# The m5 product by seven half-sized products in the middle pairs of a two-level Strassen matmul

## The chip, the cores and the metric

One core of a Trainium2 chip runs the kernel. The core has a matmul engine (TensorE, PE in the profile, with its weight loads shown as PEld), a vector engine (VectorE, DVE), a scalar engine (ScalarE, ACT), GpSimd (POOL, used here only to issue DMAs) and a sync engine (SP, which also issues DMAs). Each takes its own instructions in the order in which they were written, and waits on semaphores for the others. The metric is the device time of one execution in microseconds (us).

## The reference

```python
def setup_inputs():
    m, k, n = 4096, 4096, 4096      # all float32, standard normal

def reference(a, b, bias):
    return np.tanh(np.matmul(a, b) + bias)
```

A 4096 x 4096 x 4096 matrix product, a bias for each column, and tanh.

## The kernel before

**First level.** Data is held as fp16, sums in fp32 in PSUM. The output is cut into blocks of 256 rows by 1024 columns. There are sixteen row blocks and four column blocks c = 0 to 3. One such block is an *item* n. Each item is a 2 x 2 Strassen scheme in the Winograd form with seven products of 128 rows, 512 columns and half of the inner dimension (2048). The left operands are the quarters a11, a12, a21, a22 of the item's rows and the differences s1, s2, s5, s6, s7 of two quarters each. The right operands are the blocks b11, b22 and the sums d1, d3, d4, e6, e7. The products are m2 = s2 b11, m5 = s5 b22, m3 = a11 d3, m1 = s1 d1, m4 = a22 d4, m6 = s6 e6, m7 = s7 e7 (`PRODUCTS`). A whole product is 16 matmuls of 128 x 128 weights by 512 columns (function `whole`).

**Second level.** Two neighbouring items p = n and q = n + 1 use the same right operand. Their two left operands, one above the other, with the inner dimension and the columns halved, are again a 2 x 2 scheme. It has seven products of 8 matmuls with 256 columns each, in place of two whole products (32 matmuls with 512 columns). A product that is taken so I call *by seven halves*. It needs five differences of left halves, called lefts (`left`, tiles `h`, four buffers in turn), on VectorE. Its right operands are two quarters of the first-level operand and five forms d1, d3, d4, e6, e7 made from its quarters. `group0`, `group1` and `group2` issue two, three and two of the seven products (`multiply`). Between them ScalarE copies a part out of PSUM (`third`, tile `x`, one buffer), and VectorE makes one sum (the function that `group0` returns, the middle sum) and two differences (the function that `group1` returns). `seed` writes zeros with ScalarE into a half of a PSUM bank, since these matmuls add to what stands there.

**The stages.** In column block 2 the last eight items and in block 3 the last ten run in pairs, in an order written out by hand (`four`, and `last_four` for the very last pair). I call them four-product pairs, since m2, m3, m4 and m6 are taken by seven halves in them. Block 2 has the first pair, two middle pairs, and the leaving pair, in which m6 is whole because its operands are being replaced for block 3. Block 3 has the first pair, three middle pairs, and the last pair. In the last pair alone m5 is by seven halves too; forms of b22 for it are made during the pairs before (`pull_four` with `M5_AT`, and `twice_right` at the end of `four`). In a first, middle or leaving pair m5, m1 and m7 are whole.

**Queues.** Forms of m2 and m6 lie in DRAM and are loaded through GpSimd's DMA queue (tile `form`). Six buffers go round: when a product has used a form (`let_go`), `pull_four` issues the load of the next one. The quarters of the next pair are fetched on SP's queue from a DRAM copy (`fetch`, a<-scratch), each into the buffer that this pair's quarter leaves. Results are stored from SP as well (`store`). The fp32 tiles `ds` and `s` have two buffers each, `o` has three. PSUM has eight banks: d, c, z and w for p and for q.

**The end of a pair before.** The last whole m7 (of q) is followed by `ds -= z`, the seed of z for the next q, the fetch of a12, the tanh of ds and its store, all written before the next pair's first group.

Of the kernel before, what the change touches and what calls it, by code (L numbers as in the profile page):

```python
# [8 lines left out]
P = 128  # L9
# [72 lines left out]
M5_AT = {"d3": (2, 13), "d4": (3, 13)}  # L82
M5_REST = 3
# [30 lines left out]
def kernel(  # L114
# [84 lines left out]
    def beginning(n):  # L199
        return begins.get(items[n][0], len(items))  # L200
# [560 lines left out]
    free, held, placed, left_count, resting = [], {}, {}, [0], []  # L761

    def pull_four():
        for i in range(len(resting)):
            resting[i][0] -= 1
        while resting and resting[0][0] <= 0:
            free.append(resting.pop(0)[1])
        if queue and free and queue[0][0] == "m5":
            what, name = queue.pop(0)
            tag = free.pop(0)  # L770
            pool = spare if tag == "sum" else bops
            rights[what, name] = pool.tile([P, TP, NB // 2], fp16, name="form", tag=tag)
            twice_right(what, name)
            forms[what, name] = dram.tile([P, TP, NB // 2], fp16, name=f"form_m5_{name}")
            nc.gpsimd.dma_start(out=forms[what, name], in_=rights.pop((what, name)))
            resting.append([M5_REST, tag])
            return
        while queue and free and queue[0][0] != "m5":
            what, name = queue.pop(0)
            tag = held[what, name] = free.pop(0)  # L780
            pool = spare if tag == "sum" else bops
            rights[what, name] = pool.tile([P, TP, NB // 2], fp16, name="form", tag=tag)
            nc.gpsimd.dma_start(out=rights[what, name], in_=forms[what, name])  # L783

    def let_go(n, what, name):
        tag = held.pop((what, name))
        c = items[n][0]
        if c < NC - 1 and not queue and tag != "sum":
# [17 lines left out]
    def pair_of(n, what):  # L806
        return (bank(i, 0, TWO[what][2]) for i in (n, n + 1))
# [26 lines left out]
    def group0(n, what):  # L834
        p, q = pair_of(n, what)
        multiply(n, what, p[:, HALF[1]], "s5", (1, 1))
        multiply(n, what, q[:, HALF[0]], "s2", (0, 0))
# [21 lines left out]
    def whole(n, left_, right, parts=None):  # L859
        at = by_four(aset[n][left_])  # L860
        for to, half in parts or ((bank(n, 0, "z"), ds(0, NB)),):
            for t in range(T):
                nc.tensor.matmul(  # L863
                    to[:, half], at[:, t // TB, t % TB], bop[right, t // TB][:, t % TB, half],
                    start=False, stop=t == T - 1, skip_group_check=True,
                )

    def four_sum(n, name, leave=False, over=None):
# [4 lines left out]
        upper = (n - beginning(n)) % 2 == 0  # L873
        st = aset[n]
        if leave:
            st[name] = wide.tile([P, T, P], fp16, name=name, tag="wide")
        elif over is not None:
            st[name] = st[over] if over in QUADS else bops.tile([P, T, P], fp16, name=name, tag=over)
        elif name == "s7":
            st[name] = st["a12"]  # L880
        elif upper and name in ("s2", "s1", "s6") and (n, name) != (beginning(n), "s2"):
            st[name] = side[:, :, ds(NB if name == "s6" else 0, NB)].rearrange(
                "p a (b m) -> p a b m", m=P
            )
        elif name == "s6":
            st[name] = bops.tile([P, T, P], fp16, name="s6", tag="e6_1")
        else:
            st[name] = sums.tile([P, T, P], fp16, name=name, tag="sum")
        tt(by_four(st[name]), by_four(st[x]), by_four(st[y]), SUB)

    def seed(n, where, half):
        nc.scalar.copy(bank(n, 0, where)[:, HALF[half]], zeros)

    def add21(n):
        st = state.setdefault((n, 0), {})
        st["ds"] = temps.tile([P, NB], fp32, name="ds", tag="ds")
        tt(st["ds"], bank(n, 0, "z"), bias_bc[:, :NB], ADD)

    def add12(n):
        st = state[n, 0]  # L900
        st["s"] = temps.tile([P, NB], fp32, name="s", tag="sc")
        tt(st["s"], bank(n, 0, "z"), bias_bc[:, NB:], SUB)
# [10 lines left out]

    def four(n):
        c = items[n][0]
        p, q, m = n, n + 1, n + 2
        more = m in fours
        leave = not more
        pair = {i: items[i][1][0] for i in (p, q)}

        seed(p, "c", 1)
        seed(q, "c", 0)
        if leave:
            give_back(c, 0)
        w = group0(n, "m4")
        left(n, "m4", "s1")
        w()
        left(n, "m2", "s1")
        w = group0(n, "m2")
        if leave:  # L930
            give_back(c, 1)
        left(n, "m4", "s7")
        w()
        left(n, "m4", "s6")
        w = group1(n, "m4")
        left(n, "m2", "s7")
        w()
        if n > beginning(n):
            four_sum(p, "s5")
        w = group1(n, "m2")  # L940
        left(n, "m2", "s6")
        w()
        if n == beginning(n):
            four_sum(p, "s5")
        group2(n, "m4")
        if leave:
            give_back(c, 5)
        left(n, "m3", "s5")
        group2(n, "m2")
        if leave:  # L950
            give_back(c, 6)
        left(n, "m3", "s2")
        add21(p)
        add12(p)
        w = group0(n, "m3")
        four_sum(p, "s6", leave)
        w()
        add21(q)
        add12(q)
        left(n, "m3", "s1")  # L960
        four_sum(q, "s6", leave)
        fetch(m, "a21")
        if more:
            fetch(m + 1, "a21")
        four_sum(q, "s5")
        if leave:
            give_back(c, 7)
        whole(p, "s5", "b22")
        tt(state[p, 0]["s"], bank(p, 0, "z"), state[p, 0]["s"], SUB)
        for i in (p, q):  # L970
            tt(state[i, 0]["ds"], state[i, 0]["ds"], bank(i, 0, "d"), ADD)
            result(state[i, 0]["ds"], pair[i], 1, c, 0)
        if leave:
            give_back(c, 8)
        w = group1(n, "m3")
        if leave:
            give_back(c, 9)
        if more:
            seed(p, "d", 1)
            seed(q, "d", 0)  # L980
        left(n, "m3", "s7")
        left(n, "m3", "s6")
        w()
        four_sum(p, "s1")
        four_sum(p, "s7", leave)
        fetch(m, "a22")
        fetch(m, "a11")
        if leave:
            fetch(m, "a12")
        whole(q, "s5", "b22")  # L990
        if leave:
            give_back(c, 10)
        tt(state[q, 0]["s"], bank(q, 0, "z"), state[q, 0]["s"], SUB)
        if not leave:
            seed(p, "w", 1)
            seed(q, "w", 0)
        group2(n, "m3")
        if leave:
            give_back(c, 11)
        if not leave:  # L1000
            left(n, "m6", "s5")
            left(n, "m6", "s2")
        for i in (p, q):
            tt(state[i, 0]["s"], bank(i, 0, "c"), state[i, 0]["s"], ADD)
            result(state[i, 0]["s"], pair[i], 0, c, 1)
        four_sum(q, "s1")
        four_sum(q, "s7")
        if more:
            fetch(m + 1, "a22")
            fetch(m + 1, "a11")  # L1010
        whole(p, "s1", "d1")
        if leave:
            give_back(c, 12)
        tt(bank(p, 0, "c"), state[p, 0]["s"], bank(p, 0, "z"), SUB)
        if leave:
            whole(q, "s1", "d1")
            tt(bank(q, 0, "c"), state[q, 0]["s"], bank(q, 0, "z"), SUB)
            give_back(c, 13)
            for i in (p, q):
                whole(i, "s6", "e6", ((bank(i, 0, "c"), ds(0, NB)),))  # L1020
                result(bank(i, 0, "c"), pair[i], 1, c, 1)
                give_back(c, 14 if i == p else 16)
                whole(i, "s7", "e7")
                if i == p:
                    asum(m, "s2")
                tt(state[i, 0]["ds"], state[i, 0]["ds"], bank(i, 0, "z"), SUB)
                nc.scalar.activation(state[i, 0]["ds"], state[i, 0]["ds"], TANH)
                store(state[i, 0]["ds"], pair[i], 0, c, 0)
                give_back(c, 15 if i == p else 17)
            asum(m, "s5")  # L1030
            for k in range(18, 29):
                at_slot(SLOTS * m + k - 18, give_back, c, k)
            return
        w = group0(n, "m6")
# [740 lines left out]
```

## Time and profile before

| | us |
|---|---|
| three runs | 1532.35, 1534.38, 1531.41 |
| their median | 1532.35 |
| the profiled execution | 1531.29 |
| its span, first to last instruction | 1529.6 |

The four-product stages of the profiled execution, by start of each pair:

| column block | first pair | middle pairs | leaving or last pair |
|---|---|---|---|
| 2 | about 929.8 | 974.98, 1020.15 | 1065.32 (leaving, to 1111.3) |
| 3 | 1301.5 | 1346.67, 1391.85, 1437.02 | 1482.19 (last) |

The granted clock of TensorE is full throughout. How to read the views: "busy" is the time in which an engine executes, a share of the span; a matmul's row is longer than its place in the stream, since matmuls overlap, so their price is read from the chain of waits, which merges them into stretches. A row of a timeline has start, length, engine, line, operation, output<-input, shapes, count, and in brackets the idle time before it and what ended it. In rows of DMA issues the last number is the time from issue to landing.

### The profile page before, as it was taken

To read this page: it belongs to the slowest core of one execution; us is meant where nothing else is said; L and a number is where in the kernel's file an instruction comes from. 1 tells how busy PE (TensorE), PEld (TensorE's weight loads), DVE (VectorE), ACT (ScalarE), POOL (GpSimd) and SP (SyncE) were. 2 spreads that over 40 slices of the span, in tenths; PEclk is the share of its full clock that TensorE was granted. 3 is DMA by queue.
4 is the path that set the end of the run, shared out by engine and by line. 5 is a ranking of instruction groups with operands and counts; after the bars stand their busy time and mean duration, and the time that the engine had idled before them with its cause. 6 is when DMAs were issued, how large, how long until landed. Compare 5 with 4: busy or idle time off the path is not lost.

```text
span 1529.6 us, 22760 instructions
## 1 busy us (share of the span) xinstructions
PE 1524.3 (100%) x8541; PEld 834.4 (55%) x8541; DVE 1225.5 (80%) x1641; ACT 337.0 (22%) x677; POOL 475.5 (31%) x860
## 2 busy tenths in 40 slices
PE   9999999999999999999999999999999999999999
PEld 4444444444445666544444556766644555777766
DVE  6789877777987776777798877888669977888898
ACT  3432111111221122111122112222122211222222
POOL 7775543334513231343550121111123001111210
DMA  9999998999979998999996878988979657888984
GB/s 177 183 212 256 279 239 214 229 210 228 192 210 295 265 281 264 240 255 239 221 195 183 278 265 316 331 302 296 322 243 200 186 190 240 307 303 322 326 304 173
DMA packets 205778, 381.39 MB, mean 249 GB/s; under 512 B 25058, under 2 KB 104162, under 8 KB 205668
## 3 DMA queue, kind: packets, MB, share of 16 engines
q0 software_dynamic: 117872, 194.30, 55.8%
q1 hardware_dynamic: 87124, 185.31, 35.6%
q8 instruction: 67, 1.10, 0.3%
q10 hardware_dynamic: 672, 0.33, 0.1%
q14 instruction: 43, 0.35, 0.1%
HBM read 324.01 MB, written 141.56 MB: 304 GB/s over the span
## 4 chain that ended last, share of the span: by engine, by line
PE 95%; issue 2%; DMA 1%; POOL 1%; DVE 0%; ACT 0%; POOLq 0%; DVEq 0%
PE ps L465 58%; PE ps L825 14%; PE ps L863 12%; PE ps L640 6%; PE ps L1424 4%; DMA form<-form_m 1%; DMA land<-in_a_dram 0%; DMA side<-in_b_dram 0%; POOL b L368 0%; POOL land L1465 0%; POOL form L783 0%; POOL side L1513 0%; POOL form_m L725 0%; POOL first L1493 0%; DVE s L144 0%
## 5 line engine op out<-in xcount | busy, mean ns | idle before, releaser
L465 PEld LDWEIGHTS <-s 128*128 128x128 f16 x2256 | 220.8, 98 | 260.2 <-DVE s L144 0.2
L465 PEld LDWEIGHTS <-a 128*128 128x128 f16 x1984 | 194.1, 98 | 230.7
L465 PE MATMUL ps<-b,s 128*128 128x512 f16 x1204 | 274.7, 379 | 0.0
L144 DVE TENSOR_TENSOR s<-a,a 128x2048 f16<-128x2048 f16 (+1 forms) x190 | 228.5, 1208 | 14.0 <-DMA a<-scratch 12.7
L465 PE MATMUL ps<-e,a 128*128 128x512 f16 x964 | 219.7, 379 | 0.0
L465 PE MATMUL ps<-d,a 128*128 128x512 f16 x896 | 202.5, 379 | 0.0
L268 DVE STREAM_TRANSPOSE a<-nat 128x1024 f16<-128x1024 f16 (+2 forms) x202 | 175.0, 909 | 9.9 <-PE ps L465 8.3
L825 PEld LDWEIGHTS <-h 128*128 128x128 f16 x1440 | 140.8, 98 | 27.4 <-issue 0.4
L465 PE MATMUL ps<-d,s 128*128 128x512 f16 x688 | 155.5, 379 | 0.0
L783 POOL DMA_DIRECT2D form<-form_m x119 | 63.0, 529 | 273.1 <-PE ps L825 240.6
L240 POOL DMA_DIRECT2D nat<-in_a_dram x176 | 93.0, 533 | 133.0 <-DVE a L268 58.2
L368 POOL DMA_DIRECT2D b<-in_b_dram x192 | 103.4, 543 | 84.5 <-DVE a L268 31.1
L144 DVE TENSOR_TENSOR a<-a,a 128x2048 f16<-128x2048 f16 x88 | 106.9, 1215 | 0.0
L485 ACT ACTIVATE o<-ps 128x512 f32<-128x512 f32 x94 | 56.4, 600 | 187.1 <-issue 107.0
L825 PE MATMUL ps<-form,h 128*128 128x256 f16 x688 | 83.8, 273 | 0.2 <-DMA form<-form_m 0.2
L640 PEld LDWEIGHTS <-h 128*128 128x128 f16 x680 | 66.5, 98 | 16.7
L725 POOL DMA_DIRECT2D form_m<-stage x15 | 8.2, 548 | 199.9 <-DVE stage L144 199.9
L863 PEld LDWEIGHTS <-s 128*128 128x128 f16 x448 | 43.8, 98 | 47.8
L144 DVE TENSOR_TENSOR ps<-ps,x 128x256 f32<-128x256 f32 x106 | 45.6, 431 | 29.9 <-PE ps L825 18.1
L825 PE MATMUL ps<-d,h 128*128 128x256 f16 x576 | 68.8, 273 | 0.0
L144 DVE TENSOR_TENSOR h<-a,a 128x1024 f16<-128x1024 f16 x99 | 66.4, 683 | 1.4 <-PE ps L825 1.3
L144 DVE TENSOR_TENSOR ps<-cs,ps 128x512 f32<-128x512 f32 x43 | 29.5, 693 | 41.6 <-PE ps L465 40.2
(185 smaller groups left out, 1958.1 us busy)
## 6 DMA issues: line engine op xcount, KB each, us to landing
a<-scratch SPq DMA_DIRECT2D x140, 512.0 KB, 5.4
form<-form_m POOLq DMA_DIRECT2D x119, 512.0 KB, 6.2
out_dram<-o SPq DMA_DIRECT2D x223, 256.0 KB, 5.3
nat<-in_a_dram POOLq DMA_DIRECT2D x288, 128.0 KB, 7.2
scratch<-a SPq DMA_DIRECT2D x48, 512.0 KB, 7.0
b<-in_b_dram POOLq DMA_DIRECT2D x160, 128.0 KB, 6.0
scratch<-a SPq DMA_DIRECT2D x32, 256.0 KB, 6.1
cast<-in_b_dram POOLq DMA_DIRECT2D x64, 128.0 KB, 9.1
```

What stands on the lines that cost most here:

```text
L144: nc.vector.tensor_tensor(out=out_, in0=in0, in1=in1, op=op)
L240: nc.gpsimd.dma_start(out=tl[ds(q * QP, QP), :, :], in_=src.rearrange("(mb p) k -> p mb k", p=QP),)
L268: nc.vector.transpose(dst[:, ds(b0 * tb, n * tb), :].rearrange("P (b t) (mb p) -> P mb b t p", t=tb, p=QP), src[:, :, ds(b0, n), :].rearra ...
L368: nc.gpsimd.dma_start(out=dst[ds(q * QP, QP), ds(t, nt)], in_=src)
L465: nc.tensor.matmul(st[where], at, bt, start=(what == "m2" or n < LEAD and what == "m1") and i == 0, stop=i == len(ts_) - 1, skip_group_che ...
L485: nc.scalar.activation(o, src, TANH)
L640: nc.tensor.matmul(to, at, bt, start=False, stop=t == TP - 1, skip_group_check=True)
L725: nc.gpsimd.dma_start(out=forms[what, name], in_=stage)
L783: nc.gpsimd.dma_start(out=rights[what, name], in_=forms[what, name])
L825: nc.tensor.matmul(to, at, bt, start=False, stop=t == TP - 1, skip_group_check=True)
L863: nc.tensor.matmul(to[:, half], at[:, t // TB, t % TB], bop[right, t // TB][:, t % TB, half], start=False, stop=t == T - 1, skip_group_che ...
L1424: nc.tensor.matmul(mb[m % 4, j], aq[m, kt // T][:, kt % T, :], right(kt, j), start=fresh and kt == k0, stop=stop and kt == k1 - 1, skip_gr ...
```

## The change

In middle pairs m5 becomes a product by seven halves, like m2, m3, m4 and m6. `four` now writes the order of every pair, and `last_four` is gone.

- *Which pairs.* `x` and `y` name the two late products of a pair, x in bank d and y in bank w. In first and middle pairs x is m6 and y is m5; in the leaving and the last pair x is m5 and y is m6. In the first pair y is still whole m5 (`if first`), in the leaving pair both x and y are whole.
- *Forms of b22.* They are made once in the first pair of each block (`form`, `m5_form`) and stay. d4, d1 and d3 get buffers of their own. e6 and e7 are written over two quarters of b22 itself, after the first pair's whole m5. In block 2 these two quarters are moved to DRAM earlier, and back at the start of the leaving pair (`move("m5", ...)`). The forms made by `pull_four` (`M5_AT`) go.
- *Order in a middle pair.* m4 and m2 interleaved, m3's group 0, m6's group 0, m3's group 1, m6's group 1, m3's group 2, whole m1 of q, m6's group 2, m5's group 0, whole m1 of p, m5's group 1, whole m7 of p, m5's group 2, whole m7 of q. Before: m4 and m2 interleaved, m3's group 0, whole m5 of p, m3's group 1, whole m5 of q, m3's group 2, whole m1 of p, m6's group 0, whole m1 of q, m6's group 1, whole m7 of p, m6's group 2, whole m7 of q.
- *Where sums lie.* Differences of quarters are kept in the quarters' own buffers or in two halves A and B of `side` (`home`).
- *Left-over work.* What closes a pair is no longer written at its end. It goes on a list, `left_over`: `close` (`ds -= z` of q, the seed of z, the fetch of a12), then the tanh and store of ds of p, s of p, s of q and ds of q. The next pair takes it off at four places with `more`: the first two entries after m4's group 0, one after m2's group 0, one after m4's group 1, the last after m2's group 1.
- *Full-width work.* `take_d` reads m4 from d with the bias, and z is added later; `take_c` reads c with the bias; `take_z` writes s - z to `o`; `take` adds or subtracts m6 or m5. There are sixteen of these fp32 instructions of 512 columns in a middle pair, as before.

The diff, cut to the routine's middle pair and the functions it calls:

```diff
-M5_AT = {"d3": (2, 13), "d4": (3, 13)}
-M5_REST = 3
...
     def between(n, what):
-        return {
-            "m2": bank(n, 0, "c")[:, HALF[0]], "m4": bank(n + 1, 0, "c")[:, HALF[1]],
-            "m3": bank(n, 0, "w")[:, HALF[0]], "m5": bank(n, 0, "w")[:, HALF[0]], "m6": bank(n + 1, 0, "w")[:, HALF[1]],
-        }[what]
+        i, where, half = {
+            "m2": (n, "c", 0), "m4": (n + 1, "c", 1), "m3": (n, "w", 0),
+        }.get(what, (n + 1, "w", 1) if homes.get(what) == "d" else (n, "c", 0))
+        return bank(i, 0, where)[:, HALF[half]]
...
+    def m5_form(name):
+        if name not in OVER:
+            pool, tag = (bops, "e6_1") if name == "d4" else (sums, "sum")
+            rights["m5", name] = pool.tile([P, TP, NB // 2], fp16, name="form", tag=tag)
+        twice_right("m5", name)
...
+    left_over = []
+
+    def more(calls):
+        for f in left_over[:-(-len(left_over) // calls)]:
+            f()
+            left_over.pop(0)
...
+        x, y = ("m5", "m6") if last or leave else ("m6", "m5")
+        mine = {x: "d", y: "w"}
...
+        def end(name, i, r, j):
+            nc.scalar.activation(st[i][name], st[i][name], TANH)
+            store(st[i][name], pair[i], r, c, j)
+
+        def take(what, i, later=False):
+            to = bank(i, 0, mine[what])
+            if what == "m6":
+                tt(st[i]["o"], st[i]["o"], to, ADD)
+                ready = ("o", i, 1, 1)
+            else:
+                tt(st[i]["ds"], st[i]["ds"], to, SUB)
+                tt(st[i]["s"], to, st[i]["s"], ADD)
+                ready = ("s", i, 0, 1)
+            if later:
+                left_over.append(lambda: end(*ready))
+            else:
+                end(*ready)
...
+        def take_d(i):
+            st[i]["ds"] = temps.tile([P, NB], fp32, name="ds", tag="ds")
+            tt(st[i]["ds"], bank(i, 0, "d"), bias_bc[:, :NB], ADD)
...
         w = group0(n, "m4")
+        more(4)
         left(n, "m4", "s1")
         w()
         left(n, "m2", "s1")
         w = group0(n, "m2")
         left(n, "m4", "s7")
         w()
+        more(3)
+        if not last:
+            make("s6", p)
         w = group1(n, "m4")
         left(n, "m4", "s6")
...
         w()
+        more(2)
         left(n, "m2", "s7")
+        if not first and not last:
+            make("s6", q)
         w = group1(n, "m2")
         left(n, "m2", "s6")
         w()
...
+        more(1)
         group2(n, "m4")
         left(n, "m3", "s5")
+        left(n, "m3", "s2")
...
+        for i in (p, q):
+            take_d(i)
...
         group2(n, "m2")
...
+            seeds("d")
+            if not first:
+                seeds("w")
+        if not leave:
+            left(n, x, "s5")
         w = group0(n, "m3")
+        if not leave:
+            left(n, x, "s2")
...
         left(n, "m3", "s1")
         w()
+        if not leave:
+            w2 = group0(n, x)
+            left(n, x, "s1")
+            w2()
...
+        form("d4")
+        form("d1")
+        one_whole("m1", q)
+        for i in (p, q):
+            make("s6" if last else "s5", i)
+        if not last:
+            fetch(m, "a21")
+            fetch(m + 1, "a21")
+        group2(n, x)
+        if first:
+            one_whole(y, p)
+            one_whole(y, q)
+        else:
+            left(n, y, "s5")
+            left(n, y, "s2")
+            w = group0(n, y)
+        for i in (q, p):
+            take_c(i)
+        make("s1", p)
+        make("s7", p)
+        take_z(q)
+        if not first:
+            left(n, y, "s1")
+            w()
+        make("s7", q)
+        if not last:
+            fetch(m, "a22")
+            fetch(m + 1, "a22")
+        form("d3")
+        one_whole("m1", p)
+        take(x, q)
...
+        left(n, y, "s7")
+        w = group1(n, y)
+        left(n, y, "s6")
+        take_z(p)
         w()
+        take(x, p)
+        if not last:
+            fetch(m + 1, "a11")
+        one_whole("m7", p)
+        if not last:
+            seeds("d")
+            seeds("c")
+            left(m, "m4", "s5")
+            left(m, "m4", "s2")
+            four_sum(m, "s2", "A")
+            four_sum(m + 1, "s2", "B")
+        group2(n, y)
+        tt(st[p]["ds"], st[p]["ds"], bank(p, 0, "z"), SUB)
...
+        one_whole("m7", q)
+
+        def close():
+            tt(st[q]["ds"], st[q]["ds"], bank(q, 0, "z"), SUB)
+            seed(q, "z", 0)
+            fetch(m + 1, "a12")
+
+        left_over.insert(0, close)
+        left_over.append(lambda: end("ds", p, 0, 0))
+        take(y, p, True)
+        take(y, q, True)
+        left_over.append(lambda: end("ds", q, 0, 0))
```

More of the change, by code (lines that the diff above doesn't have):

```diff
@@ L759, in bring_block @@
         nc.gpsimd.dma_start(out=new_bop(name, blk), in_=blocks[c, name, blk])
-    free, held, placed, left_count, resting = [], {}, {}, [0], []
+    free, held, placed, left_count, homes, wanted, reserved = [], {}, {}, [0], {}, [], []
     def pull_four():
[L764 to L778, printed above, removed]
+        if queue and free:
             what, name = queue.pop(0)
@@ L956, in four @@
[L956 to L1033, printed above, removed]
@@ new lines, in four @@
+        if not last:
+            seed(p, "z", 1)
+            fetch(m, "a12")
+            left(m, "m2", "s5")
+            left(m, "m2", "s2")
+        else:
+            for to, half in ((bank(q, 0, "z"), LAST[0]), (bank(p, 0, "c"), LAST[1])):
+                tt(to[:, half], bank(q, 0, "z")[:, half], st[q]["ds"][:, half], SUB)
+            end("ds", p, 0, 0)
+            for i in (p, q):
+                take(y, i)
+            o = st[q]["ds"]
+            for to, half, on in (
+                (bank(q, 0, "z"), LAST[0], nc.sync), (bank(p, 0, "c"), LAST[1], nc.scalar)
+            ):
+                whole(q, "s7", "e7", ((to, half),))
+                nc.scalar.activation(o[:, half], to[:, half], TANH, scale=-1.0)
+                on.dma_start(
+                    out=out[ds(2 * pair[q] * P, P), ds(c * NCW + half.start, half.size)],
+                    in_=o[:, half],
+                )
+            return
```

371 lines of the change are left out of this document (171 added, 200 removed), and 2 rows, old and new, of the table BACK.

## The prediction

> **What bounds the kernel now.** I read the page's totals first, then the waits of TensorE, then the chain of waits in one four-product pair, then the busy time pair by pair. The page:
>
> ```profile
> span 1529.6 us, 22760 instructions
> PE 1524.3 (100%) x8541; PEld 834.4 (55%) x8541; DVE 1225.5 (80%) x1641; ACT 337.0 (22%) x677; POOL 475.5 (31%) x860
> ```
>
> TensorE is busy all the way. Of its waits only one lies in the stages that the change touches:
>
> ```profile
> PE ps L825 <- DMA form<-form_m: 0.2, 1, 0.2
> ```
>
> So nothing can be won here by removing a wait; only fewer or shorter matmuls shorten the kernel, and any new wait of TensorE lengthens it. The chain through the second pair of the last column block (start, length, what):
>
> ```profile
> 1346.67 13.97 PE ps L825 x128
> 1360.65 3.45 PE ps L863 x16
> 1364.10 2.62 PE ps L825 x24
> 1366.72 3.45 PE ps L863 x16
> 1370.17 1.75 PE ps L825 x16
> ```
>
> L825 are the half-wide matmuls: 128 in 13.97 us, 0.109 us each, so a half-sized product of 8 takes 0.873 us. L863 are the full ones: 16 in 3.45 us. This gives the gain of the change. Next, busy time by pair (columns: window, then its length and PE, then PEld, DVE, ACT, POOL with instruction counts):
>
> ```profile
> 1301.50:1346.67 45.17, 45.17 (x323) 31.30 (x321) 38.15 (x58) 11.10 (x26) 7.93 (x15) 1.00 0.87 314
> 1346.67:1391.85 45.18, 45.18 (x323) 31.32 (x321) 38.33 (x58) 11.09 (x26) 7.39 (x14) 1.00 0.85 301
> 1437.02:1482.19 45.17, 45.17 (x323) 31.32 (x321) 41.66 (x64) 11.09 (x26) 7.92 (x15) 1.00 0.88 315
> ```
>
> VectorE is the second engine: 38.33 of 45.18 us in a plain pair, 6.85 idle, and 41.66 in the pair that also makes forms of b22. This is where the change puts its new work.
>
> **TensorE, the gain.** In a middle pair m5 is now two whole products, 2 x 3.45 = 6.90 us. It becomes seven half-sized ones, 7 x 0.873 = 6.11. That is 0.79 us less, and the pair takes 44.38 us instead of 45.17. Middle pairs are two in column block 2 and three in block 3, so -3.95 us. The first and leaving pairs keep whole m5, the last pair had seven halves already. Each m5 also loads 56 weights instead of 32; weight loads fill 31.3 of 45.2 us beside the matmuls, so 24 more are not on the path.
>
> The Trainium skill ("TensorE: Matmul & The Clock Gate", section "Back-to-back issue gap") says that in a real stream of weight loads and matmuls the pace is about 81 ns at 128 columns and about 131 ns at 512. An estimate on the line between those two figures is 98 ns at 256 columns, by which seven halves (56) would take 5.5 us against 4.2 for 32 full ones and the five pairs would lose 6.5 us. The trace disagrees: 109 ns and 216 ns in the rows above.
>
> **VectorE, the price.** Each kind takes its place in the row of instructions by the distance from start to next start:
>
> ```profile
> 1369.34 1.22 DVE L144 TENSOR_TENSOR side<-a,a 128x2048 f16<-128x2048 f16 x1
> 1370.47 1.22 DVE L144 TENSOR_TENSOR a<-a,a 128x2048 f16<-128x2048 f16 x1
> 1371.60 0.68 DVE L144 TENSOR_TENSOR s<-ps,s 128x512 f32<-128x512 f32 x1
> 1372.20 0.68 DVE L144 TENSOR_TENSOR h<-side 128x1024 f16<-128x1024 f16 x1
> 1372.80 0.68 DVE L144 TENSOR_TENSOR h<-s 128x1024 f16<-128x1024 f16 x1
> ...
> 1377.56 0.43 DVE L144 TENSOR_TENSOR ps<-x,ps 128x256 f32<-128x256 f32 x1
> 1377.90 0.68 DVE L144 TENSOR_TENSOR h<-s,side 128x1024 f16<-128x1024 f16 x1
> ...
> 1383.30 0.90 DVE L144 TENSOR_TENSOR ps<-ps,x 128x256 f32<-128x256 f32 x2 [1.99 <-PE ps L825]
> 1384.11 0.68 DVE L144 TENSOR_TENSOR h<-a 128x1024 f16<-128x1024 f16 x1
> ```
>
> A sum of 2048 takes 1.13, a left of 1024 or an fp32 one of 512 0.60, the middle sum of a second-level product 0.34, its two closing differences 0.81. Seven halves of m5 need five lefts, one middle sum and two differences: 3.00 + 0.34 + 0.81 = 4.15 us more. The full-width fp32 instructions stay 16: take_d, adding z, take_c, take_z, m6, the last z, two each, and four for m5. So 66 instructions and 38.33 + 4.15 = 42.5 us in 44.38: 1.9 us idle where there were 6.85. In the first pairs five forms of b22 at two instructions, 10 x 0.60 = 6.0, make 38.15 + 6.0 = 44.2 of 45.17. I cost this at nothing because it still fits and the following pair can absorb a small lag; if it does not fit, whatever is over goes onto TensorE. The form work that leaves the other pairs of block 3 (64 instead of 58 instructions above) was hidden, and gains nothing.
>
> **The order, walked.** The first seven groups, up to m3's s5 and s2, keep their places, so a pair's start of today serves as clock (0 = 1346.51):
>
> ```profile
> 1346.51 1.91 PE L825 MATMUL ps<-d,h 128*128 128x256 f16 x16
> 1347.75 0.63 ACT L1071 ACTIVATE ds<-ds 128x512 f32<-128x512 f32 x1
> 1348.28 0.66 ACT L892 CAST ps<-zeros 128x256 f32<-128x256 f16 x2
> 1348.40 0.33 SPq L476 DMA_DIRECT2D out_dram<-ds  x1
> 1350.01 1.04 PE L825 MATMUL ps<-g,h 128*128 128x256 f16 x8
> 1350.20 0.37 ACT L831 COPY x<-ps 128x256 f32<-128x256 f32 x1 [0.96 <-PE ps L825]
> 1352.89 0.90 DVE L144 TENSOR_TENSOR ps<-ps,x 128x256 f32<-128x256 f32 x2 [0.46 <-PE ps L825]
> 1353.91 0.37 ACT L831 COPY x<-ps 128x256 f32<-128x256 f32 x1 [2.21 <-DVE ps L144]
> 1360.48 3.62 PE L863 MATMUL ps<-b,s 128*128 128x512 f16 x16
> ```
>
> Now the last tanh of the previous pair's ds (item q) stands at 1.2 us, its store at 1.9. The change puts it at the end of a list of left-over work, after the copy at 1353.91, which is 7.40. The tanh then runs 7.7 to 8.35 and its store is issued at 8.4. This is a new wait: take_d(q) of the new pair writes the same one of two "ds" buffers and must wait for that store to land. Counting instructions from m4's differences at 6.4 (0.81, a left, a sum, a left, 0.81, two lefts, take_d(p)): 6.4 + 0.81 + 0.60 + 1.13 + 0.60 + 0.81 + 1.20 + 0.60 = 12.1 us, when take_d(q) could start. Behind it stand m6's first left and all that follows on VectorE. At 13.97 (1360.48 above) TensorE wants m6's s5 product in place of the whole m5, and needs that left: take_d(q) + 0.60 + 0.68. So the left is in time if the store lands within 4.3 us of its issue. Landing times of stores (last column):
>
> ```profile
> out_dram<-o SPq DMA_DIRECT2D x2, 256.0 KB, 2.8
> ...
> form<-form POOLq DMA_DIRECT2D x2, 512.0 KB, 4.9
> out_dram<-o SPq DMA_DIRECT2D x2, 256.0 KB, 4.4
> ...
> form<-form_m POOLq DMA_DIRECT2D x5, 512.0 KB, 6.8
> form<-form_m_d POOLq DMA_DIRECT2D x2, 512.0 KB, 6.7
> out_dram<-o SPq DMA_DIRECT2D x2, 256.0 KB, 4.8
> ...
> form<-form_m POOLq DMA_DIRECT2D x1, 512.0 KB, 7.0
> out_dram<-o SPq DMA_DIRECT2D x2, 256.0 KB, 7.4
> a<-scratch SPq DMA_DIRECT2D x1, 512.0 KB, 7.2
> ```
>
> These are the stores around 1374, 579, 1499 and 1390: 2.8 us with no form in flight, 4.4 and 4.8 with forms in flight, 7.4 behind a fetch on SP's queue as well. At 8.4 us three forms of m2 and m6 are being loaded and no fetch is near, so I take 4.8: TensorE waits 0.5 us. Ends: 0 (4.4 and less) and 3.1 (7.4). It strikes pairs that follow a middle pair and run a second-level product there: one in block 2, three in block 3 with the last. 4 x 0.5 = +2.1 us.
>
> The seed of z for q moves likewise, from the end of a pair into the next one behind its first copy: the copy starts 0.19 after the product (1350.20 against 1350.01), at 1.94; two seeds in 0.66 us are 0.3 apart and take 0.37, so copy and seed end at 2.61; the m2 product that needs it is due at 2.62. With the signal's way I take 0.08 in five pairs, +0.4; ends 0 and 0.2 each. In the last pair three VectorE steps (0.60 and the split pair of about 1.0) now lie between m7 of p and the split m7 of q, covered by 1.75 us of m6: +0.2, ends 0 and 0.5.
>
> What costs nothing, and its cover: fetches move within SP's queue, but even at the 7.2 us of the last row each is there before its reader, but for a22 of q (second rival). m6's forms are called 14 us earlier; the tightest is freed at 7.0, called at 7.4 and used at 14.8, so it may take 7.4 us where the forms called at that place now take 5.5 in the median (they would add waits of POOL's queue only). Moving two quarters of b22 out and back in block 2 is eight SP transfers, the return needed 17 us later. ScalarE has two copies more and two fewer.
>
> ```profile
> form<-form_m POOLq DMA_DIRECT2D x3, 512.0 KB, 5.5
> ```
>
> Sum: -3.95 + 2.1 + 0.4 + 0.2 = -1.25 us. The profiled execution took 1531.29 us, so 1530.0. The three runs' median is 1.06 above it and their lowest 0.12; I add 0.5 and say 1530.5. About 0.2% (3.1 us) is what a measurement of this kernel can tell from no change, so this is "same".
>
> **The rivals.** First, the store lands in 4.3 us or less and the wait does not exist: -3.95 + 0.6 = -3.35, 1527.9 (1528.4 as median), faster by 0.22%. For it: the 4.4 row; against it: other stores of the same list go out 3 us ahead on that queue.
>
> Second, slower: VectorE becomes the bound. Its waits within a pair must stay under 1.9 us; today they are 6.85. In the new order three are forced: m6's middle sum waits for a copy (about 0.5), m5's differences for a product (0.7), take_d(q) (up to 1). If a22 of q lands late (SP issues it when s7 of q is done, near 32.8, and the left that reads it is due at 37.9, so 5.1 us) or lag adds up, everything over 1.9 falls on TensorE in five pairs. From 1.4 us over, 3.3 in all, the gain is lost and 0.2% more. At 3.6 in all, half of today's waits: 5 x 1.7 - 3.95 = +4.5, 1535.8. Against it: a lagging VectorE finds its inputs ready, and most of the 6.85 is such slack.
>
> Third: the store lands in 6.1 us or more: 4 x 1.8 - 3.35 = +3.9, 1535.2. Fourth, two half-wide matmuls cost more than one full one, so that m5 gains nothing: with the waits above 1531.3 + 2.7 = 1534.0; the 13.97 us row denies it. This is the rule of the Trainium skill's "Back-to-back issue gap" from above.
>
> **How the numbers follow.** Forecast 0.37, first rival 0.35, second 0.17, third 0.10, fourth 0.01. So faster 0.35, same 0.38, slower 0.27. The range runs from the gain with no wait, 1531.3 - 3.95 + 0.3 = 1527.6, to the second and third rivals' 1536; the forecast alone spans 1529 to 1533.
>
> **What would show it.** Right: middle pairs of 44.4 us plus a gap of half a microsecond before m6's s5, named as VectorE h, with VectorE waiting there for out_dram<-ds. First rival: no such wait. Second: VectorE over 43 us busy in a pair, waits of TensorE in several places. It would also be wrong if first pairs grow past 45.2 or a form is waited for.

## The result, and the profile after

The changed kernel takes 1537.62 us (median of six runs, 1535.69 to 1541.08) against 1531.59 us of the kernel before in the same session. The ratio is 1.004, with a 95% interval of 1.0026 to 1.0054: the change costs 0.4%, about 6 us. The prediction was 1530.5 us and its range ended at 1536.0.

The profiled execution took 1535.69 us, the lowest of the six, so the trace shows 4.4 us of the loss. Two lines of its page:

```profile
span 1534.0 us, 23098 instructions
PE 1522.5 (99%) x8661; PEld 846.2 (55%) x8661; DVE 1249.9 (81%) x1693; ACT 336.0 (22%) x681; POOL 473.5 (31%) x856
```

TensorE is busy 1.8 us less than before (1524.3) and the span is 4.4 us longer: most of the loss is waiting. A second, smaller part, a lower clock, hides in the busy time and is shown below. The waits of TensorE (total, times, longest) that lie in the changed stages:

```profile
PE ps L811 <- DVE h L142: 6.5, 3, 2.4
PE ps L811 <- DVE ps L142: 0.3, 1, 0.3
```

The one wait that stood here before, 0.2 us for a form, has become four for VectorE (line 811 is the half-wide matmul, 142 VectorE's sums). Which pairs they strike is seen in busy time by pair, from the second pair of block 2 on (window, length and PE, PEld, DVE, ACT, POOL, then the granted clock):

```profile
973.81:1018.29 44.48, 44.48 (x346) 33.58 (x345) 42.46 (x67) 11.02 (x27) 7.40 (x14) 1.00 0.92 325
1018.29:1066.48 48.19, 46.24 (x346) 34.41 (x345) 42.15 (x68) 11.30 (x28) 7.40 (x14) 0.96 0.84 285
1066.48:1112.98 46.50, 46.16 (x298) 28.87 (x296) 31.28 (x47) 8.85 (x18) 7.33 (x13) 1.00 0.93 323
1303.19:1348.49 45.30, 45.30 (x323) 31.21 (x321) 42.64 (x66) 9.69 (x24) 7.93 (x15) 1.00 0.87 309
1348.49:1392.87 44.38, 44.38 (x346) 33.66 (x345) 42.48 (x68) 11.04 (x27) 7.40 (x14) 1.00 0.94 327
1392.87:1439.83 46.96, 44.58 (x346) 33.56 (x345) 41.96 (x68) 11.49 (x28) 7.40 (x14) 1.00 0.85 291
1439.83:1486.56 46.73, 44.58 (x346) 33.56 (x345) 41.96 (x68) 11.48 (x28) 7.41 (x14) 1.00 0.86 293
```

In the kernel before, block 2 from its second pair on stood like this in the chain of waits (start, length, what; the last row is the stage after the block):

```profile
974.98 13.97 PE ps L825 x128
...
1020.15 13.97 PE ps L825 x128
...
1065.32 13.97 PE ps L825 x128
...
1111.29 4.75 PE ps L465 x22
```

So its pairs took 45.17, 45.17 and 45.97 us, and those of block 3 45.17 or 45.18. Against them:

| pair | difference, us |
|---|---|
| block 2: second (first middle one) | -0.69 |
| block 2: third (second middle one) | +3.02 |
| block 2: leaving | +0.53 |
| block 3: first | +0.13 |
| block 3: second (first middle one) | -0.80 |
| block 3: third, fourth (middle ones behind a middle one) | +1.79, +1.56 |

These sum to +5.5. The last pair adds 0.05, up to its last 32 full matmuls (41.07 us against 41.02). The second pair of block 2 begins 1.17 us earlier than before, so that 4.4 remain. The gain of m5 is there in the two middle pairs that run behind a first pair. In the three that run behind another middle pair it is eaten by one gap each. The timeline of the first of these (start, length, what, and in brackets the idle time before it with what ended it; the pair starts at 1018.12):

```profile
1025.55 0.37 ACT L817 COPY x<-ps 128x256 f32<-128x256 f32 x1 [1.88 <-DVE ps L142]
1025.81 0.64 ACT L934 ACTIVATE ds<-ds 128x512 f32<-128x512 f32 x1
1026.47 0.33 SPq L474 DMA_DIRECT2D out_dram<-ds  x1
1032.89 0.69 DVE L142 TENSOR_TENSOR ds<-ps,bias_bc 128x512 f32<-128x512 f32 x1 [2.53 <-DMA out_dram<-ds]
```

And TensorE's first wait in each of the three (timeline of PE):

```profile
1034.24 2.42 PE L811 MATMUL ps<-form,h 128*128 128x256 f16 x16 [1.95 <-DVE h L142]
1409.25 1.92 PE L811 MATMUL ps<-form,h 128*128 128x256 f16 x16 [2.38 <-DVE h L142]
1455.98 1.92 PE L811 MATMUL ps<-form,h 128*128 128x256 f16 x16 [2.15 <-DVE h L142]
```

The last tanh of the previous pair's ds (item q) now stands behind the copy, its store is issued 8.35 us after the pair's start, take_d(q) waits for it 2.53 us on VectorE, and m6's s5 product waits for the left behind take_d(q). The chain of waits has the same place:

```profile
1026.47 6.32 DMA out_dram<-ds
...
1033.50 0.69 DVE h L142
...
1034.24 10.57 PE ps L811 x80
```

The store takes 6.3 us to land, 6.8 and 6.5 in block 3. The last row is a second loss: 80 half-wide matmuls are 80 x 0.109 = 8.73 us, and here they take 10.57. Two windows, the gap at the end of the first (granted clock is the third number from the end):

```profile
1032.10:1035.51 3.41, 1.46 (x14) 1.15 (x13) 2.62 (x5) 1.29 (x4) 0.00 (x0) 1.00 1.03 417
1035.51:1038.92 3.41, 3.41 (x18) 2.45 (x17) 2.63 (x6) 0.90 (x3) 1.06 (x2) 0.50 0.67 225
```

From 1.3 us after the gap of 1.95 us on, the granted clock is 0.50 for 3.41 us, then full again. After the gaps of 2.38 and 2.15 us in block 3 it does not fall, and the same 80 take 8.91. So 0.18 us of the 10.57 is paid behind every gap, and the lower clock costs 10.57 - 8.91 = 1.66 us, about half of 3.41 and nearly as much as the gap: with 44.40 for a middle pair without a gap, 48.19 = 44.40 + 1.95 + 0.18 + 1.66.

### The profile page after: what moved, and what is told of

Its sections match the earlier page's. It is cut to its first block, busy times and chain, and to the rows that moved or that the text cites. A ratio compares the mean times of both kernels' runs of the same rounds, so it can differ in the third digit from the quotient of the medians.

```text
span 1534.0 us, 23098 instructions
## 1 busy us (share of the span) xinstructions
PE 1522.5 (99%) x8661; PEld 846.2 (55%) x8661; DVE 1249.9 (81%) x1693; ACT 336.0 (22%) x681; POOL 473.5 (31%) x856
## 4 chain that ended last, share of the span: by engine, by line
PE 97%; DMA 2%; DVE 1%; ACT 0%; issue 0%; ACTq 0%; DVEq 0%
PE ps L463 60%; PE ps L811 14%; PE ps L850 10%; PE ps L638 7%; PE ps L1443 5%; DMA out_dram<-ds 2%; DMA coarse<-in_a_dram 0%; DVE ps L142 0%; DVE h L142 0%; DVE s L142 0%; ACT ds L934 0%; PE warm L1503 0%; ACT x L817 0%; PE spread L426 0%; PE tp L1544 0%
## 5 line engine op out<-in xcount | busy, mean ns | idle before, releaser
L463 PEld LDWEIGHTS <-s 128*128 128x128 f16 x2256 | 220.7, 98 | 260.2 <-DVE s L142 0.2
L463 PEld LDWEIGHTS <-a 128*128 128x128 f16 x1984 | 194.1, 98 | 230.6
L142 DVE TENSOR_TENSOR s<-a,a 128x2048 f16<-128x2048 f16 (+1 forms) x154 | 185.3, 1206 | 16.6 <-DMA a<-scratch 15.3
L811 PEld LDWEIGHTS <-h 128*128 128x128 f16 x1640 | 160.4, 98 | 34.6 <-DVE h L142 8.7
L142 DVE TENSOR_TENSOR a<-a,a 128x2048 f16<-128x2048 f16 x118 | 142.6, 1215 | 0.0
L811 PE MATMUL ps<-form,h 128*128 128x256 f16 x728 | 89.5, 274 | 6.5 <-DVE h L142 6.5
L142 DVE TENSOR_TENSOR h<-a,a 128x1024 f16<-128x1024 f16 x123 | 82.0, 682 | 0.1
L638 PEld LDWEIGHTS <-h 128*128 128x128 f16 x680 | 66.5, 98 | 16.6
L850 PEld LDWEIGHTS <-a 128*128 128x128 f16 x448 | 43.2, 98 | 46.5
L142 DVE TENSOR_TENSOR ps<-ps,x 128x256 f32<-128x256 f32 x116 | 49.9, 430 | 20.5 <-PE ps L638 8.7
```

Of the source, the lines that this page charges most:

```text
L142: nc.vector.tensor_tensor(out=out_, in0=in0, in1=in1, op=op)
L463: nc.tensor.matmul(st[where], at, bt, start=(what == "m2" or n < LEAD and what == "m1") and i == 0, stop=i == len(ts_) - 1, skip_group_che ...
L638: nc.tensor.matmul(to, at, bt, start=False, stop=t == TP - 1, skip_group_check=True)
L811: nc.tensor.matmul(to, at, bt, start=False, stop=t == TP - 1, skip_group_check=True)
L850: nc.tensor.matmul(to[:, half], at[:, t // TB, t % TB], bop[right, t // TB][:, t % TB, half], start=anew and t == 0, stop=t == T - 1, skip ...
```

## The experiments

Three readings of the loss were set against each other. A: the late store of the ds of q holds its buffer, and take_d(q) behind it. B: VectorE, 42 of 44.4 us busy, has become the bound and the store is only where the lag shows. C: the traffic on the DMA engines has grown, and what moves late suffers whatever it is.

**The store early again.** The tanh and store of the ds of q go to the second place of the list of left-over work; nothing else changes.

```diff
         left_over.append(lambda: end("ds", p, 0, 0))
+        left_over.append(lambda: end("ds", q, 0, 0))
         take(y, p, True)
         take(y, q, True)
-        left_over.append(lambda: end("ds", q, 0, 0))
```

> The changed kernel with one move: the tanh and store of ds of q are second of the stores on the left-over list instead of last, so the store is issued about 3.8 us earlier (near 4.6 in the pair instead of 8.4). Theory A (take_d(q) waits for this store to land, and that is all that was lost): with a landing of 6.5 us the store is down at 11.1, before take_d(q) is due at 12.1; VectorE waits for no store, TensorE waits for no left in the middle pairs, middle pairs take 44.4 us, granted clock full; against the kernel before -3.95 + 0.6, ratio 0.998 (about 1528.3 us where before takes 1531.6). Theory B (VectorE, at 42.5 of 44.4 us busy, is the new bound and the store only the place where it shows): the waits of TensorE move to other products and at least half of the 7 us stays, ratio 1.001 or more.

It took 1527.97 us, ratio 0.9977 (0.9968 to 0.9985), 3.5 us faster than before. Two middle pairs, the second behind a middle one:

```profile
974.81:1019.20 44.39, 44.39 (x347) 33.61 (x345) 42.59 (x68) 11.03 (x27) 7.40 (x14) 1.00 0.93 325
1019.19:1063.60 44.41, 44.41 (x347) 33.61 (x345) 42.04 (x67) 11.56 (x28) 7.40 (x14) 1.00 0.90 304
```

VectorE is as busy as in the changed kernel and TensorE waits for nothing in them: B falls. One wait is left, in the second pair of block 3, where the pair before is a first pair with its own list:

```profile
1360.33 1.92 PE L811 MATMUL ps<-form,h 128*128 128x256 f16 x16 [1.25 <-DVE h L142]
```

It is of the same kind. The chain there shows that pair's store on its way for 8.4 us:

```profile
1350.52 8.43 DMA out_dram<-ds
```

**The store late, from another buffer.** The tanh stays where the change put it, but writes to one of the o buffers and is stored from there, so that take_d(q) has no store to wait for.

```diff
-        left_over.append(lambda: end("ds", q, 0, 0))
+        left_over.append(lambda: result(st[q]["ds"], pair[q], 0, c, 0))
```

> The changed kernel with the store of ds of q left where it is, but its tanh written to an o buffer, so that the ds buffer is free when ScalarE has read it (about 8.4 us in the pair) and not when the store has landed (about 15). Theory A: as the early store, no wait for a store before take_d(q), ratio 0.998. Theory B: ratio 1.001 or more. A third theory C, that the late store harms by its traffic (forms or fetches land later beside it), expects no gain here but a gain from the early store.

1528.03 us, ratio 0.998 (0.9971 to 0.9989). The same store is issued at the same place behind the same transfers and is as slow (6.53, 6.66 and 6.67 us to land in the three pairs behind a middle pair), and TensorE waits for nothing there. It is the buffer, so A, and not the traffic, C. One wait of 0.99 us is left behind the first pair of block 3, where the early store had left 1.25; this edit does not touch that pair's list.

**The store later still.** Six copies of zeros onto zeros ahead of the late tanh on ScalarE (the output does not change).

```diff
-        left_over.append(lambda: end("ds", q, 0, 0))
+        def idle_first():
+            for _ in range(6):
+                nc.scalar.copy(zeros, zeros)
+            end("ds", q, 0, 0)
+
+        left_over.append(idle_first)
```

> The changed kernel with six small ScalarE copies (zeros onto zeros, 128 x 256) ahead of the late tanh of ds of q: the store goes out about 1.8 us later, ScalarE has nothing else to do there. Theory A: each of the three waits of about 2.2 us in middle pairs grows by 1.8, the leaving pair's 0.3 to about 2, the last pair gets one of about 1.5: 1.8 x 4 + 1.5, some 8 us more than the changed kernel, ratio to before about 1.009, more if the granted clock drops after longer gaps. Theory B: below 1.006, since the copies cost VectorE nothing.

1557.97 us, ratio 1.0176 (1.016 to 1.0191), about twice the loss that was expected. The six copies took 2.6 us, not 1.8, and the clock took its share. TensorE's waits, and the window in which the clock is low at the longest gap:

```profile
PE ps L811 <- DVE h L142: 17.0, 5, 5.5
PE ps L811 <- DVE ps L142: 2.6, 1, 2.6
```

```profile
1415.29:1422.12 6.83, 4.57 (x22) 3.26 (x23) 3.96 (x8) 1.66 (x5) 1.06 (x2) 0.50 0.25 91
```

At the two longest gaps the clock is half for 6.83 us, twice as long as above; the first part of that lies in the gap itself. The chain has 11.11 us for the 80 matmuls here, 2.2 more than the 8.91 at full clock. A holds in sign and place, but its price per microsecond of delay was too low.

**Three copies.** The same with `range(3)`, to see whether gaps of less than 3 us cost only their own length.

> As the late store, with three ScalarE copies ahead of it instead of six: half of the delay, 0.9 us. Six cost not the 8 us expected but 20 over the changed kernel, with a granted clock of 0.50 to 0.65 for some 4 us after each gap of 3.9 us and more. If the clock falls only after gaps beyond some length between 2.4 and 3.9 us, gaps of about 3.1 here are a test: with the clock full, 4 x 0.9 + 0.7 us over the changed kernel, ratio about 1.0065; with the clock falling after most of them another 2 us each, ratio about 1.012.

1554.26 us, ratio 1.0147 (1.0131 to 1.0162): not half of the loss. The store is issued 1.2 us later than in the changed kernel, and it lands later by more. The same store in block 3, in the chain with three copies,

```profile
1407.13 8.57 DMA out_dram<-ds
```

and with six:

```profile
1408.74 7.37 DMA out_dram<-ds
...
1417.55 11.11 PE ps L811 x80
```

The pair starts 0.3 us earlier in the first of these runs, so the store is issued 1.3 us earlier there and lands at 18.1 us of the pair, against 18.2. In the other pairs that follow a middle pair it lands between 0.8 us earlier and 0.8 later with three copies than with six. Two forms are called on POOL's queue at 11.8 and 12.7 us of the pair and would be moving beside it; that they set the time of its landing is argued, not shown. Most gaps were longer than 3.1 us, up to 5.4. Of the two between 1 and 3.1 us the one of 1.81 us leaves the clock full, and the one of 3.01 us, in the last pair, halves it for 3.41 us. So a gap of about 3 us can cost more than its own length.

**What lies ahead on SP's queue.** In the changed kernel the issues before the late store are those of two s results, 3.7 us ahead at the most (issues by kind: KB each, median us to landing):

```profile
out_dram<-s SPq DMA_DIRECT2D x2, 256.0 KB, 6.5
...
out_dram<-ds SPq DMA_DIRECT2D x1, 256.0 KB, 6.3
```

Reading S: the store is slow because it queues behind these two. To test it, the tanh and store of both s go behind m3's middle sum, after the store of ds, which stays as late as it was.

```diff
+        while behind:
+            behind.pop(0)()
...
+        behind.extend(left_over[2:])
+        left_over[2:] = [lambda: None, lambda: None]
         left_over.append(lambda: end("ds", q, 0, 0))
```

> The changed kernel with the store of ds of q as late as there, but the tanh and store of s of p and of q after it (behind m3's middle sum) instead of 2.8 and 3.7 us ahead of it. Why did the store take 6.3 to 6.8 us to land where 4.8 was taken? Theory S (it lands behind the two s stores on SP's own queue): it lands in 4.8 or less, TensorE's wait is at most 0.5 us a pair, ratio 0.998 to 0.9995. Theory F (the forms in flight on the other queue hold it): it still lands in 6 or more, waits of about 2 us stay, ratio 1.003 or more.

1528.72 us, ratio 0.9985 (0.9976 to 0.9994). The chain and the timeline of the pair that lost most:

```profile
1027.77 4.65 DMA out_dram<-ds
```

```profile
1032.51 0.69 DVE L142 TENSOR_TENSOR ds<-ps,bias_bc 128x512 f32<-128x512 f32 x1 [0.85 <-DMA out_dram<-ds]
1033.85 0.83 PE L811 MATMUL ps<-form,h 128*128 128x256 f16 x6 [0.27 <-DVE h L142]
```

With neither s store ahead it lands in 4.65 us instead of 6.3, with the forms called at the same places, and the gap is 0.27 us instead of 1.95. In the two such pairs of block 3 it lands in 3.97 and 3.83 us instead of 6.75 and 6.52. So the two s stores ahead of it cost it about 1.7 to 2.8 us in the middle pairs, as S says. Two things stay open. The edit takes the place on SP's queue and the bytes on the DMA engines away together, and does not tell which of them counts. And the two stores are not enough by themselves: in the last pair of the changed kernel they stand as far ahead (3.7 and 2.8 us), and the store lands in 3.24 us; POOL's queue calls five forms there in the pair's first 13 us, where it calls seven in a middle pair.

**m5 whole, the store early.** The early store of the first experiment, but m5 as two whole products in all middle pairs; the forms of b22 are made in the pair before the last only, and nothing is moved out and back. It measures the gain of the seven products alone.

```diff
         first, last = n == begins[c], m == len(items)
         leave = m not in fours and not last
+        alone = not leave and not last
...
-            if first:
+            if m + 2 == len(items):
                 m5_form(name)
...
-        if first:
+        if alone:
             one_whole(y, p)
             one_whole(y, q)
```

> The early store, but m5 whole in all middle pairs (as in the first pair), the forms of b22 made only ahead of the last pair, no move of quarters: the new order without the smaller product. Theory A: 5 x 0.79 us above the early-store kernel, level with the kernel before, ratio 0.9995 to 1.0010, VectorE about 38 of 45.2 us busy in middle pairs. Theory B: faster than the early-store kernel, as it takes 4.15 us of VectorE's work from each middle pair.

1532.36 us, ratio 1.0007 (0.9998 to 1.0015): as before. A middle pair:

```profile
1020.09:1065.26 45.17, 45.17 (x322) 31.28 (x321) 38.16 (x58) 10.22 (x24) 7.40 (x14) 1.00 0.87 302
```

45.17 against 44.39 and 44.41 of the first experiment: 0.77 us a pair, and the two medians are 4.4 us apart, where five pairs make 3.9. The half-microsecond more is less than either interval (about 1.3 us each way).

**All left-over stores from other buffers.** The first experiment with every left-over ds, of p and of q, stored through the o buffers.

```diff
-            left_over.append(lambda: end("ds", q, 0, 0))
-            left_over.append(lambda: end("ds", p, 0, 0))
+            left_over.append(lambda: result(st[q]["ds"], pair[q], 0, c, 0))
+            left_over.append(lambda: result(st[p]["ds"], pair[p], 0, c, 0))
...
-        left_over.append(lambda: end("ds", p, 0, 0))
+        left_over.append(lambda: result(st[p]["ds"], pair[p], 0, c, 0))
+        left_over.append(lambda: result(st[q]["ds"], pair[q], 0, c, 0))
```

> The early store, and the tanh of every left-over ds (p and q, after first pairs too) written to an o buffer, so that no take_d waits for any store. Theory A: the one wait left with the early store (1.25 us in the pair after the first one of block 3, where the list has another order) goes; all middle pairs 44.4 us; ratio to before 0.9970 to 0.9980 (-3.95 + 0.4 us). If VectorE's load is near its limit it would show here as waits of TensorE for lefts without any store in the chain, and a ratio above 0.998.

1527.55 us, ratio 0.9975 (0.9966 to 0.9985), the lowest of all here, though not told apart from 1527.97. No wait for a ds store is left, and what remains in the changed stages is small:

```profile
PE ps L811 <- DMA form<-form_m: 1.2, 2, 0.8
...
PE ps L811 <- DVE ps L142: 0.3, 1, 0.3
```

**The changed kernel twice more**, to see what differs between its executions.

> The changed kernel once more, for a second profile. In its first profile three gaps of TensorE of 1.95 to 2.4 us cost 2.2 to 2.6 each, and one of them a further 1.8 through a lower granted clock after it. If that loss comes and goes from run to run, this is what spreads the six times over 1535.7 to 1541.1: the span should be about 1532.2 plus 1.8 for each gap that is followed by a lower clock, 0 to 3 of them, with gaps of the same length. If instead the landing of the store spreads them, the gaps differ in length by more than 1 us between profiles.

> The changed kernel a third time, expected as the second: gaps of about 2 to 2.4 us at the same three places, the span moved by 1.8 us for each lower clock behind them.

They took 1542.12 and 1543.05 us, one execution each, both above the highest of the six (1541.08). They are the second and third profiled executions of this kernel. The chains in block 3 have in the second

```profile
1401.65 8.24 DMA out_dram<-ds
1411.33 11.56 PE ps L811 x80
1452.74 6.35 DMA out_dram<-ds
1460.53 10.57 PE ps L811 x80
```

and in the third

```profile
1403.12 8.38 DMA out_dram<-ds
1412.94 10.57 PE ps L811 x80
1453.37 6.50 DMA out_dram<-ds
1461.32 10.57 PE ps L811 x80
```

where the first had 6.75 and 6.52 us of landing and 8.91 us for the 80 matmuls both times. The same store lands in 6.75, 8.24 or 8.38 us, so the gap before the matmuls is 2.38, 3.86 or 4.01; and the second gap, 2.15, 1.98 and 2.13 us in the three executions, lowers the clock in two of them. Both vary. Why the landing varies is open. In block 2 the chain of the third execution has

```profile
1035.14 8.91 PE ps L811 x80
```

behind a gap of 2.08 us, where 1.95 had cost 1.66 us of clock in the first.

What decides about the clock can be read from the traces. In each of them the times between changes of the granted clock are whole multiples of 3.413 us (in block 3 of the second execution 6.827, 44.373 and 3.413 us: 2, 13 and 1). So a trace can be divided into steps of 3.413 us, counted from the first change that it records, and the idle time of TensorE can be summed in each step. The clock changes in nine traces, those of the changed kernel and of all its variants but the one with m5 whole. There 13 steps at full clock hold 1.95 us of idle time or more, and after every one of them the clock is half for the next step. After all the others, some 3960 with at most 1.92 us, it stays full. The gap of 1.95 us lies whole in one step (the two windows of the first execution above are this step and the next). The gap of 2.38 is divided into 0.70 and 1.68, and that of 2.12 in block 2 of the second execution into 1.92 and 0.20 (idle time is the length of the window less PE):

```profile
1031.09:1034.50 3.41, 1.49 (x14) 1.09 (x12) 1.14 (x2) 0.40 (x3) 0.53 (x1) 1.00 1.04 417
1034.50:1037.92 3.42, 3.21 (x30) 2.89 (x31) 3.14 (x7) 1.63 (x6) 1.06 (x2) 1.00 0.65 249
```

So by these traces a gap of 1.95 to 3.9 us (twice 1.95, so that one of two steps must hold 1.95) loses the clock or not by where it falls on the steps, and nothing in this kernel sets that. A pair after a first pair also loses in some executions: 0, 1.12 and 2.04 us in the second pair of block 3, whose store there lands in 6.90, 8.30 and 9.23 us in the three executions.

## Why the prediction was wrong

The step that failed is the landing of the moved store, 4.8 us in the sum and 6.3 to 8.4 measured, and with it the wait of 0.5 us a pair. A second term, the clock behind a gap, was put at nothing without a reason.

- **The new wait** was foreseen with its place, its victim and its cause: the store was put at 8.4 us of the pair and was issued at 8.35; the waiting instruction is take_d(q); TensorE stops before m6's s5. The prediction's condition, in time if the store lands within 4.3 us, also held: 4.65 us gave a gap of 0.27, 6.3 one of 1.95.
- **Its price** was wrong. Of the rows 2.8, 4.4, 4.8 and 7.4 the prediction took 4.8, a store with forms in flight, because no fetch was near, and so 0.5 us. The two s stores ahead on SP's queue, which it named itself against the first rival, belong in the same sum: in middle pairs the store takes 6.3 to 8.4 us with them, and 3.8 to 4.65 without them, about the number taken. Per pair 1.95, 2.38 and 2.15 us came instead of 0.5. The row of 7.4, stores with something of their own queue ahead, was the nearer one, and the moved store itself, at its old place, takes 6.0 to 9.2 us to land in the profile before. This is the third rival's case (6.1 us or more, 1535.2 us), which was given 0.10.
- **How many pairs** it strikes was four at 0.5. It was three in the profile; in the last pair, with two forms fewer called, the store landed in 3.2 us (4.5 and 4.7 in the two later executions) and the gap there was at most 0.3. The leaving pair of block 2 lost 0.34 us, 0.84 and 0.95 in the later executions, through m3's middle sum behind the same kind of store (6.70 us), which was not in the sum.
- **The clock after a gap** is missing from the prediction. A gap was costed at its length; behind it came 0.18 us each time and, where the clock fell, 1.66 to 2.65 us more (10.57 or 11.56 for the 80 matmuls, against 8.91). In the profiled execution -3.95 + 6.82 of waits + 0.70 behind four gaps + 1.66 of clock = +5.23, of 5.6 measured in these stages. That execution, at 1535.69, lies just inside the range. What puts the median beyond it has no profile of its own; in the two later executions it is a longer landing, a further wait and more steps at half clock.
- **The gain of m5**, 0.79 us a pair, is right: middle pairs without a gap take 44.38 to 44.48 us, predicted 44.38, and the kernel with m5 whole lies 4.4 us behind the one with the early store (predicted 3.95).
- **VectorE**, 42.5 us busy predicted, has 42.0 to 42.5 in the middle pairs, and it is not the bound (second rival): at 42.04 and 42.59 of 44.4, with the early store, TensorE waits for nothing.
- **The first pairs** were expected at 44.2 us of VectorE in an unchanged 45.17; it is 42.64 in block 3, and the pair takes 45.30. The 1.6 us too many is an error of the count (58 instructions became 66, not 68). The pair is 0.1 us over the 45.2 that the prediction named as a sign of being wrong, and why stays open.
- **The seeds of z**, 0.08 us in five pairs: 44.38 to 44.48 us is 0 to 0.1. **The last pair**, +0.2: it was +0.05.
- **The first rival** is what the early store makes of the change: 1528.4 us as a median, and it measured 1527.97.

## What to carry to other kernels

When a store moves to a later place, look for the next writer of its source buffer, and take the landing time from a store that has the same neighbours ahead on its own queue, not only the same traffic beside it. A gap on a busy TensorE can cost more than its length: here gaps under 1.95 us cost 0.18 us more, gaps from there to 3.9 us cost that or a further 1.7 us by where they fell, and longer ones always lost the clock. Where a result can go out of either of two buffers, take the one that nothing writes soon: here that alone took the kernel from 1537.62 to 1528.03 us.

## What the runs showed that was not expected

- **The clock after short gaps.** In one kernel gaps of 1.95, 1.98 and 2.13 us halved the granted clock for 3.41 us and cost 1.66 us each, and gaps of 2.04, 2.08, 2.12, 2.15 and 2.38 us did not. What counts is the idle time within one step of 3.413 us: at 1.95 us or more the next step is at half clock, at 1.92 or less it is at full clock. The Trainium skill ("TensorE: Matmul & The Clock Gate", section "HAM oscillation — how this bites in real kernels") gives as the rule that no gap of TensorE should exceed about 3.4 us. These runs agree for the longer gaps, 3.86 to 5.48 us, which all lost the clock. For shorter ones they don't: three gaps of 1.95 to 2.13 us, and two of 2.64 and 3.01 us with the late stores, lost it too.
- **A store issued later need not land later.** With three and with six copies ahead, issued 1.3 us apart, it landed at 18.1 and 18.2 us of the pair, after 8.57 and 7.37 us.
- **The spread of a stalled kernel.** The changed kernel's six runs spread over 5.4 us. Between its three profiled executions the landing of one store (6.75 to 8.38 us) and the clock after it make a good part of the difference.
